# One fused two-block kernel: the attention modulation computed by quarters of the features instead of halves

## The chip, the cores and the metric

The kernel runs on one core of a Trainium2 chip. A core has a matrix engine (TensorE, called PE in the profile; PEld is its weight load), VectorE (DVE), ScalarE (ACT), GpSimd (POOL) and a queue processor that issues DMAs (SP). The metric is the device time of one execution in microseconds (us); the median of several runs counts.

## The reference

Two transformer blocks are computed for 256 tokens of 1024 features. The change lies in the first lines of the first block:

```
mod_x = silu(c)     @ w_ada + b_ada          # 1024 x 6144, one row for x
mod_c = silu(c_ctx) @ w_ada + b_ada          # and one for the context
sh_a, sc_a, g_a, sh_m, sc_m, g_m = split(mod_x, 6)      # the same for mod_c
hx = rmsnorm(x)   * (1 + sc_a)  + sh_a       # 256 x 1024
hc = rmsnorm(ctx) * (1 + csc_a) + csh_a      # 256 x 1024
qa, ka, va, qb, kb, vb, ga, gb = split(h @ w_in)        # for hx and for hc
```

Then come grouped-query and differential attention, an output merge, a mixture of 32 experts with 4 per token, and the second block (an mLSTM mixer, a MoBA attention mixer, and a feed-forward layer after each). Everything is float32.

## The kernel before

All weights come as one stream from HBM (`w_stream`), cut into tiles of 1 MB (128 partitions x 2048 numbers) in the order that `weight_plan` lists. SP issues the loads in that order; a load waits until one of five buffers (pool `w`) is free. A tile of `w_in` is split by `split` into two rounded parts, `whi` (ACT, L295) and `wlo` (DVE, L296), 128x1024 at a time; activations are split likewise (`hx_hi`, `hx_lo` for x, `hc_hi`, `hc_lo` for the context). A product of such parts is three PE instructions (`mm3`, L300 to L302).

The parts of `phase_a` that matter here, in the order of the code:

- `normed("x")` normalizes the token rows and transposes them on PE (L341).
- `modulation(half)` computes shift and scale of 512 of the 1024 features, for x and the context at once: 16 products (`ada_tile`, L504) of a stationary 128x32 block with `silu(c)` in column 0 and `silu(c_ctx)` in column 1. The scale goes to 32 rows of one PSUM bank and the shift to 32 others, so two 32-column groups of PE are in use; the sum over the eight 128-row blocks of `w_ada` is made in PSUM. ACT copies the result to `mod` (L619), PE transposes it (L511), and DVE adds the biases and the norm gain (L625 to L627).
- `modulated(n, k2)` applies it to two blocks of 128 features: one on DVE, one on POOL (L636), then ACT and DVE split the result.
- `first(n, ts, half)` is half of the contraction of the first projections: `vb` (512 columns) and `ka` (256 columns) for four tiles of 128 tokens, of which tiles 0 and 1 are x and 2 and 3 the context.

The sequence is: half 0 of the modulation, its products with x, the normalization of the context (`normed("ctx")`), products with the context, half 1, the rest. After these first products comes the block of `w_in` columns 1280 and up (`kb`), with the tiles of the later modulations (n = 1, 2) taken as a side task. A scheduler sets the final order of the instructions on each engine from the order of the code and the dependencies; each engine works through its own list in order.

Of the kernel before, what the change touches and what calls it, by code (L numbers as in the profile page):

```python
# [9 lines left out]
F32 = mybir.dt.float32  # L10
# [3 lines left out]
AF = mybir.ActivationFunctionType  # L14
OP = mybir.AluOpType
AX = mybir.AxisListType
PSUM = bass.MemoryType.PSUM

D = 1024
T = 256  # L20
KD = D // 128
# [36 lines left out]
def weight_plan():  # L58
# [4 lines left out]
    def add(name, layer, k0, kn, c0, n, split=True):  # L63
        plan.append((name, layer, k0, kn, c0, n, split))

    def ts(name, c0, n, ktot, layer=None, side=None, per=1):
        step = min(ktot, 2048 // n)
        for k0 in range(0, ktot, step):
            add(name, layer, k0, min(step, ktot - k0), c0, n)
            for _ in range(per if side else 0):  # L70
                add(*side.pop(0), False)
# [7 lines left out]
    def ada0(half):  # L79
        for k0 in range(0, KD, 2):  # L80
            add("w_ada", None, k0, 2, half * 1024, 1024, False)

    ada0(0)
    add("w_in", None, 0, 4, 1792, 512)
    ts("w_in", 512, 256, KD)
    ada0(1)
    add("w_in", None, 4, 4, 1792, 512)
    side = [("w_ada", None, k, 1, n * 2048, 2048) for n in (1, 2) for k in range(KD)]
# [148 lines left out]
class Kernel:  # L237
# [318 lines left out]
    def phase_a(self):  # L556
# [56 lines left out]
        def modulation(half):  # L613

            ps = self.pp.tile([128, 512], F32, name="ada", tag="ada", bufs=1)
            for k0 in range(0, KD, 2):
                self.ada_tile(ps, 64 * half, k0, 2, half * 1024, 1024)
            b = mod[64 * half:64 * half + 64]
            nc.scalar.activation(b, ps[64 * half:64 * half + 64], AF.Copy)  # L619
            mt = self.mod_T(mod, 64 * half, 64)  # L620
            cc = slice(4 * half, 4 * half + 4)
            wide = lambda v: v[:, None, :].to_broadcast([128, 2, 4])
            b0 = CR["b_ada"] + 4 * half
            g0 = CR["norm_attn"] + 4 * half
            nc.vector.tensor_add(sh[:, :, cc], mt[:, :, 32:34].rearrange("p c r -> p r c"), wide(self.cols[:, b0:b0 + 4]))  # L625
            nc.vector.tensor_tensor(sc[:, :, cc], mt[:, :, 0:2].rearrange("p c r -> p r c"), wide(b1[:, cc]), op=OP.add)
            nc.vector.tensor_tensor(sc[:, :, cc], sc[:, :, cc], wide(self.cols[:, g0:g0 + 4]), op=OP.mult)  # L627
# [20 lines left out]
        wf = {}  # L648
        def first(n, ts, half):

            for t in ts:
                o = bank_ka[t // 2][:, (t % 2) * 256:(t % 2 + 1) * 256] if n == "ka" else bank_vb[t]
                for k in range(4 * half, 4 * half + 4):
                    self.mm3(o, act(t)(k), wf[n](k if n == "ka" else k - 4 * half),
                             k == 0 and (n == "vb" or t % 2 == 0), k == KD - 1)
# [3 lines left out]
        modulated("x", 1)  # L659
# [3 lines left out]
        self.hp = hp  # L663
        wf["ka"] = w.take("w_in", None, 0, KD, 512, 256)
        bank_ka = [self.bank("psd") for _ in range(2)]
        normed("ctx")
        first("ka", (0, 1), 0)
        modulated("ctx", 0)
        modulated("ctx", 1)
        first("ka", (2, 3), 0)  # L670
        w.load(self.sv, a["k_sv"].rearrange("(o n) -> o n", o=1).to_broadcast([128, NSV]))
        modulation(1)
        first("vb", (2, 3), 0)
        modulated("x", 2)
        modulated("x", 3)
        modulated("ctx", 2)
        modulated("ctx", 3)
        wf["vb"] = w.take("w_in", None, 4, 4, 1792, 512)
        first("ka", range(4), 1)
        first("vb", range(4), 1)  # L680
# [1310 lines left out]
def pack(i):  # L1991

    f = lambda n: np.asarray(i[n])
    p = {}
# [28 lines left out]
    blocks = [2, 0, 3, 1] + list(range(4, 12))  # L2023
    w["w_ada"] = f("w_ada")[0].reshape(D, 12, 512)[:, blocks].reshape(D, 6 * D)
# [50 lines left out]
```

## Time and profile before

| | us |
|---|---|
| median of 3 runs | 1837.52 |
| lowest, highest | 1836.62, 1842.04 |
| profiled execution | 1840.18 |
| its span in the trace | 1838.40 |
| PE busy | 1751.6 (95%) |
| DVE busy | 792.8 (43%) |
| ACT busy | 533.1 (29%) |
| POOL busy | 123.2 (7%) |

The profile is of one execution; times in it count from the start of its span. "Busy" is time in which an engine has an instruction in hand. On PE the instructions are pipelined: a row lasts longer than the distance to the next start. A float32 product that is not split stands as two PE records, a product of split parts and a transpose as one.

### The profile page before, as it was taken

Reading aid. Unit: us, or ns where it says so; the run is one execution under the profiler, and the core shown is the slowest. Engines: PE = TensorE matmul, PEld = TensorE weight load, DVE = VectorE, ACT = ScalarE, POOL = GpSimd, SP = SyncE. Lnnn points to the kernel's source line nnn. Section 1 sums busy time; section 2 is a strip of 40 time slices with the busy share of each in tenths; the row PEclk is TensorE's granted clock in tenths of the full one; section 3 lists DMA queues with packets and bytes.
Section 4 is the critical chain, followed back from the end, with each engine's and each line's share of the span. In section 5 each row is a group of like instructions: output and inputs, shape, how many; then the busy total and the mean of one; then the engine's idle time right before and its main releaser. Section 6 shows DMA issues by size and latency. Waiting matters only on the chain.

```text
span 1838.4 us, 24331 instructions
## 1 busy us (share of the span) xinstructions
PE 1751.6 (95%) x9995; PEld 1106.0 (60%) x9995; DVE 792.8 (43%) x1596; ACT 533.1 (29%) x826; POOL 123.2 (7%) x167
## 2 busy tenths in 40 slices
PE   8999998999993999999989999889999999999999
PEld 4867895333331333333333333338999998899997
DVE  4688864222120121212211211136676657966653
ACT  3456741010100010101001001024554444655442
POOL 1320030000000000000000000010400002310000
PEclk9999998999997999999999999989999999999999
DMA  9475485999999999999999999994355554445551
GB/s 361 161 301 194 152 351 203 425 423 425 425 426 383 417 423 425 426 426 423 426 425 424 427 424 425 426 371 165 138 184 184 184 181 169 166 149 189 184 184 69
DMA packets 62903, 563.49 MB, mean 307 GB/s; under 512 B 8139, under 2 KB 8388, under 8 KB 10308
## 3 DMA queue, kind: packets, MB, share of 16 engines
q1 hardware_dynamic: 62096, 560.72, 75.9%
q8 instruction: 80, 1.31, 0.3%
q0 software_dynamic: 416, 1.05, 0.2%
q14 instruction: 35, 0.29, 0.0%
q10 hardware_dynamic: 276, 0.13, 0.0%
HBM read 560.82 MB, written 1.05 MB: 306 GB/s over the span
## 4 chain that ended last, share of the span: by engine, by line
PE 65%; DMA 30%; DVE 3%; ACT 1%; issue 1%; POOL 0%; ACTq 0%; SPq 0%; DVEq 0%
DMA w<-in_w_stream_dram 30%; PE bk L1415 18%; PE psd L300 12%; PE psd L301 12%; PE psd L302 12%; PE ada L504 2%; PE ps L1339 1%; PE ps L1380 1%; PE bk L1410 1%; DVE wlo L296 1%; PE psT L849 1%; PE bk L302 0%; PE bk L300 0%; PE bk L301 0%; PE ps L1443 0%
## 5 line engine op out<-in xcount | busy, mean ns | idle before, releaser
L1415 PE MATMUL bk<-w,xT 128*64 128x512 f32 x2048 | 500.8, 600 | 42.6 <-DMA w<-in_w_stream_dram 42.6
L296 DVE TENSOR_TENSOR wlo<-w,whi 128x1024 fp32r<-128x1024 f32 x246 | 298.9, 1240 | 138.2 <-ACT whi L295 135.0
L1415 PEld LDWEIGHTS bk<-w,xT 128*64 128x64 f32 x2048 | 152.1, 137 | 315.3 <-issue 263.3
L295 ACT ACTIVATE whi<-w 128x1024 fp32r<-128x1024 f32 x246 | 251.4, 1053 | 197.5 <-PE psd L301 110.6
L1415 PE MATMUL bk<-w,aT 128*64 128x512 f32 x1024 | 260.5, 606 | 12.3 <-DMA w<-in_w_stream_dram 11.6
L300 PE MATMUL psd<-u_hi,whi 128*128 128x256 f32 x768 | 217.2, 283 | 0.0
L302 PE MATMUL psd<-u_hi,wlo 128*128 128x256 f32 x768 | 215.3, 280 | 0.0
L301 PE MATMUL psd<-u_lo,whi 128*128 128x256 f32 x768 | 215.3, 280 | 0.0
L1415 PEld LDWEIGHTS bk<-w,aT 128*64 128x64 f32 x1024 | 79.3, 138 | 149.8 <-issue 125.2
L302 PEld LDWEIGHTS psd<-u_hi,wlo 128*128 128x128 f32 x768 | 146.9, 191 | 0.0
L301 PEld LDWEIGHTS psd<-u_lo,whi 128*128 128x128 f32 x768 | 144.3, 188 | 0.2
L300 PEld LDWEIGHTS psd<-u_hi,whi 128*128 128x128 f32 x768 | 144.2, 188 | 0.2
L1444 ACT ACTIVATE aT<-ps 128x512 f32<-128x512 f32 x32 | 19.1, 597 | 388.6 <-PE ps L1443 388.6
L1473 DVE TENSOR_SCALAR b_gate<-bk 128x512 f32<-128x512 f32 x32 | 20.6, 686 | 246.0 <-PE bk L1410 246.0
L1474 ACT ACTIVATE b_th<-b_gate 128x1024 f32<-128x1024 f32 x16 | 16.9, 1058 | 283.2 <-DVE b_gate L1473 283.2
L1433 DVE TENSOR_SCALAR sv<-bk 128x512 f32<-128x512 f32 x32 | 22.1, 692 | 176.2 <-PE bk L1410 176.2
L1403 DVE SCALAR_TENSOR_TENSOR y_lo<-bk,wc,y_hi 128x512 fp32r<-128x512 f32 x32 | 22.6, 747 | 138.7 <-ACT y_hi L1402 138.7
L1340 DVE SCALAR_TENSOR_TENSOR xT<-ps,g_m,xT 128x256 f32<-128x256 f32 x136 | 59.7, 479 | 43.2 <-PE ps L1339 43.2
L1402 ACT ACTIVATE y_hi<-bk,wc 128x512 fp32r<-128x512 f32 x32 | 20.3, 683 | 135.6 <-PE bk L1415 122.2
L1372 POOL TENSOR_TENSOR sw<-oh,wth 128x512 f32<-128x512 f32 x8 | 8.3, 1043 | 750.5 <-PE ps L1392 599.6
L1339 PEld LDWEIGHTS ps<-ohT,y_hi 128*128 128x128 f32 x128 | 23.8, 187 | 49.6 <-DVE xT L1340 27.8
L300 PE MATMUL psd<-whi,u_hi 128*128 128x512 f32 x128 | 52.5, 410 | 0.0
(510 smaller groups left out, 2789.2 us busy)
## 6 DMA issues: line engine op xcount, KB each, us to landing
w<-in_w_stream_dram SPq DMA_DIRECT2D x291, 1024.0 KB, 10.6
w<-in_w_stream_dram SPq DMA_DIRECT2D x119, 2048.0 KB, 28.0
w<-in_w_stream_dram SPq DMA_DIRECT2D x4, 512.0 KB, 4.5
x_rows<-in_x_dram SPq DMA_DIRECT2D x2, 512.0 KB, 4.4
vb<-in_ctx_dram SPq DMA_DIRECT2D x2, 512.0 KB, 15.3
out_dram<-x_rows SPq DMA_DIRECT2D x4, 256.0 KB, 2.0
sv<-in_k_sv_dram SPq DMA_DIRECT2D x1, 572.0 KB, 10.0
b_raw<-in_b_gate_dram POOLq DMA_DIRECT2D x2, 128.0 KB, 9.2
```

The source lines that it names most:

```text
L295: self.nc.scalar.activation(hi, v, AF.Copy)
L296: self.nc.vector.tensor_sub(lo, v, hi.bitcast(F32))
L300: mm(out, a[0], b[0], start=start, stop=False, skip_group_check=True)
L301: mm(out, a[0], b[1], start=False, stop=False, skip_group_check=True)
L302: mm(out, a[1], b[0], start=False, stop=stop, skip_group_check=True)
L504: self.nc.tensor.matmul(ps[p:p + 32, :], self.cs[:, k0 + k, :], v[:, k, j * 512:(j + 1) * 512], start=k0 + k == 0, stop=k0 + k == KD - 1, ...
L1339: self.nc.tensor.matmul(o, y[:, k * 128:(k + 1) * 128], places, start=i == 0, stop=i == len(terms) - 1)
L1340: self.nc.vector.scalar_tensor_tensor(self.xT[:, k, :], o, self.g_m[:, k:k + 1], self.xT[:, k, :], op0=OP.mult, op1=OP.add)
L1403: nc.vector.scalar_tensor_tensor(y[1][:, c], dn, wc, y[0][:, c].bitcast(F32), op0=OP.mult, op1=OP.subtract)
L1415: last = mm(o[64 * i:64 * i + 64], lhs[:, k, 64 * i:64 * i + 64], v[i], start=k == 0, stop=stop, skip_group_check=True)
L1433: nc.vector.tensor_scalar(u, o, 7.0, -7.0, op0=OP.min, op1=OP.max)
L1473: nc.vector.tensor_scalar(g[:, half(hf)], o[hf], 7.0, None, op0=OP.min)
```

## The change

The modulation is computed for 256 features at a time (four quarters). A quarter is two tiles of `w_ada` with 512 columns and four row blocks each, where the 512 columns are 256 of the shift followed by 256 of the scale. The four row blocks of a tile go to the four 32-column groups of PE, so the PSUM bank holds four partial sums of both rows. ACT copies the bank; four small products with a 128x2 matrix `pick` (ones in rows 0, 32, 64, 96 for its first column and 1, 33, 65, 97 for its second) add the four partial sums and transpose at once. The columns of `w_ada` in the stream are ordered to fit. `first` works by quarters too, and the code order changes: products with x for quarter 0, then quarter 1, the normalization of the context, quarters 0 and 1 with the context, quarter 2, quarter 3.

```diff
-    def ada0(half):
-        for k0 in range(0, KD, 2):
-            add("w_ada", None, k0, 2, half * 1024, 1024, False)
+    def ada0(q):
+        for k0 in (0, 4):
+            add("w_ada", None, k0, 4, q * 512, 512, False)
     ada0(0)
     add("w_in", None, 0, 4, 1792, 512)
+    ada0(1)
     ts("w_in", 512, 256, KD)
-    ada0(1)
+    ada0(2)
     add("w_in", None, 4, 4, 1792, 512)
+    ada0(3)
...
+        pick = long.tile([128, 2], F32, name="pick")
+        nc.vector.reduce_sum(pick, self.ident.rearrange("p (g s) -> p s g", s=32)[:, 0:2, :], axis=AX.X)
-        def modulation(half):
+        def modulation(q):
             ps = self.pp.tile([128, 512], F32, name="ada", tag="ada", bufs=1)
-            for k0 in range(0, KD, 2):
-                self.ada_tile(ps, 64 * half, k0, 2, half * 1024, 1024)
-            b = mod[64 * half:64 * half + 64]
-            nc.scalar.activation(b, ps[64 * half:64 * half + 64], AF.Copy)
-            mt = self.mod_T(mod, 64 * half, 64)
+            for k0 in (0, 4):
+                v = w.take("w_ada", None, k0, 4, q * 512, 512)
+                for k in range(4):
+                    nc.tensor.matmul(ps[32 * k:32 * k + 32, :], self.cs[:, k0 + k, :], v[:, k, :], start=k0 == 0,
+                                     stop=k0 == 4, skip_group_check=True)
+            nc.scalar.activation(mod, ps, AF.Copy)
+            for c in range(4):
+                nc.tensor.matmul(ps[:, 2 * c:2 * c + 2], mod[:, c * 128:(c + 1) * 128], pick, start=True, stop=True,
+                                 skip_group_check=True)
+            mt = ps[:, 0:8].rearrange("p (c r) -> p r c", r=2)
...
         modulation(0)
         modulated("x", 0)
-        modulated("x", 1)
         wf["vb"] = w.take("w_in", None, 0, 4, 1792, 512)
         first("vb", (0, 1), 0)
+        modulation(1)
+        modulated("x", 1)
+        first("vb", (0, 1), 1)
         wf["ka"] = w.take("w_in", None, 0, KD, 512, 256)
         normed("ctx")
-        first("ka", (0, 1), 0)
-        modulated("ctx", 0)
-        modulated("ctx", 1)
-        first("ka", (2, 3), 0)
-        modulation(1)
-        first("vb", (2, 3), 0)
+        for q in range(2):
+            first("ka", (0, 1), q)
+        for q in range(2):
+            modulated("ctx", q)
+            for n in ("vb", "ka"):
+                first(n, (2, 3), q)
+        modulation(2)
         modulated("x", 2)
+        modulated("ctx", 2)
+        first("ka", range(4), 2)
+        wf["vb"] = w.take("w_in", None, 4, 4, 1792, 512)
+        first("vb", range(4), 2)
+        modulation(3)
         modulated("x", 3)
-        modulated("ctx", 2)
         modulated("ctx", 3)
-        wf["vb"] = w.take("w_in", None, 4, 4, 1792, 512)
-        first("ka", range(4), 1)
-        first("vb", range(4), 1)
+        for n in ("vb", "ka"):
+            first(n, range(4), 3)
```

How the instructions stand on the engines is shown at three places. On ACT, before, from the copy of the first modulation (`mod`) to the second; `x_rows` with `vb` as source are the squares of the context rows:

```order
L619 ACTIVATE mod<-ada 64x512
L295 ACTIVATE whi<-w 128x1024
L295 ACTIVATE hx_hi<-h 128x512
L295 ACTIVATE whi<-w 128x1024
L295 ACTIVATE hx_hi<-h 128x512
L595 ACTIVATE x_rows_121,n_ss<-vb 128x1024 x2
L295 ACTIVATE whi<-w 128x1024 x2
L601 ACTIVATE ctx_nT<-psT 128x512 x4
L295 ACTIVATE hc_hi<-h 128x512 x2
L619 ACTIVATE mod<-ada 64x512
```

And the same place on ACT in the changed kernel (L297 is the old L295, L627 the old L619, L597 the old L595):

```order
L627 ACTIVATE mod<-ada 128x512
L297 ACTIVATE hx_hi<-h 128x512
L297 ACTIVATE whi<-w 128x1024 x2
L627 ACTIVATE mod<-ada 128x512
L597 ACTIVATE x_rows_121,n_ss<-vb 128x1024
L297 ACTIVATE hx_hi<-h 128x512
L597 ACTIVATE x_rows_121,n_ss<-vb 128x1024
L297 ACTIVATE whi<-w 128x1024 x2
L603 ACTIVATE ctx_nT<-psT 128x512 x4
L297 ACTIVATE hc_hi<-h 128x512 x2
```

The first `whi` has moved behind `hx_hi`, and the second modulation's copy and `hx_hi` now stand ahead of and between the squares of the context.

On PE in the changed kernel, around the modulation of quarter 1 (L625 its products, L630 the small ones; the product ahead is the last with quarter 0, those behind are the first with quarter 1):

```order
L304 MATMUL psd<-whi,hx_lo 128x512
L625 MATMUL ada<-w,cs 32x512 x8
L630 MATMUL ada<-pick,mod 128x2 x4
L302 MATMUL psd<-whi,hx_hi 128x512
L303 MATMUL psd<-wlo,hx_hi 128x512
L302 MATMUL psd<-whi,hx_hi 128x512
```

Nothing stands between the small products and the products that need their result. Before, 24 products with `hc` that do not need the second modulation stood behind its transposes.

On PE in the changed kernel, from the modulation of quarter 2 to the first products with it:

```order
L304 MATMUL psd<-whi,hc_lo 128x256
L625 MATMUL ada<-w,cs 32x512 x8
L630 MATMUL ada<-pick,mod 128x2 x4
L625 MATMUL ada<-w,cs 32x512 x5
L302 MATMUL psd<-whi,hx_hi 128x256
L303 MATMUL psd<-wlo,hx_hi 128x256
```

Five of the eight products of quarter 3 stand behind quarter 2's small products. The other three follow behind all products of quarter 2, and the small products of quarter 3 then stand between products of the `kb` block, of which 12 have moved ahead; the first tile of the next modulation (four products that stood together) is cut into one and three.

## Rows read from the trace of the kernel before

**Rows 1.** The page: PE's line of the busy times; the chain's shares.
```profile
PE 1751.6 (95%) x9995; PEld 1106.0 (60%) x9995; DVE 792.8 (43%) x1596; ACT 533.1 (29%) x826; POOL 123.2 (7%) x167
PE 65%; DMA 30%; DVE 3%; ACT 1%; issue 1%; POOL 0%; ACTq 0%; SPq 0%; DVEq 0%
```

**Rows 2.** Stretches: length, busy us (instructions) by engine, granted clock, DMA share, GB/s.
```profile
10.00:20.00 10.00, 10.00 (x48) 3.41 (x47) 2.81 (x5) 1.79 (x3) 0.00 (x0) 1.00 1.01 420
23.20:26.70 3.50, 3.48 (x9) 2.67 (x10) 3.40 (x6) 2.91 (x5) 1.44 (x1) 0.53 0.99 414
26.70:47.00 20.30, 19.38 (x118) 12.57 (x116) 8.09 (x25) 6.41 (x11) 1.26 (x2) 1.00 0.87 339
...
200.00:320.00 120.00, 114.57 (x825) 93.29 (x824) 72.74 (x209) 50.56 (x103) 16.57 (x27) 0.96 0.64 243
320.00:1240.00 920.00, 855.72 (x3737) 321.15 (x3735) 190.96 (x364) 93.77 (x151) 12.02 (x16) 0.98 1.00 420
```

**Rows 3.** Timeline, PE: start, us, instruction, count, [idle before, what ended it].
```profile
12.44 1.53 PE L341 MATMUL psT<-ident,x_rows 128*128 128x128 f32 x12
...
13.90 6.20 PE L504 MATMUL ada<-w,cs 128*32 128x512 f32 x26
...
23.22 1.09 PE L300 MATMUL psd<-whi,hx_hi 128*128 128x512 f32 x2 [1.98 <-ACT hx_hi L295]
```

**Rows 4.** Timeline, ACT, DVE and POOL, from the first modulation's copy on.
```profile
20.13 0.59 ACT L619 ACTIVATE mod<-ada 64x512 f32<-64x512 f32 x1 [5.53 <-PE ada L504]
20.62 1.04 ACT L295 ACTIVATE whi<-w 128x1024 fp32r<-128x1024 f32 x1
...
21.27 0.17 DVE L625 TENSOR_TENSOR sh_a<-ps,cols 128x8 f32<-128x8 f32 x1 [6.90 <-PE ps L511]
...
21.82 2.82 POOL L636 TENSOR_SCALAR h<-x_nT,sc_a,sh_a 128x256 f32<-128x256 f32 x2 [20.75 <-DVE sc_a L627]
22.53 0.63 ACT L295 ACTIVATE hx_hi<-h 128x512 fp32r<-128x512 f32 x1 [0.87 <-POOL h L636]
22.57 1.21 DVE L296 TENSOR_TENSOR wlo<-w,whi 128x1024 fp32r<-128x1024 f32 x1
```

**Rows 5.** Line L636: its POOL instructions, ns shortest/median/longest.
```profile
L636 POOL TENSOR_SCALAR h<-x_nT,sc_a,sh_a x4: 581/770/2147, 21.8 to 48.6; 128x256 f32<-128x256 f32 x4
```

**Rows 6.** Timeline, PE: part of the second modulation, and its transposes.
```profile
35.67 3.63 PE L504 MATMUL ada<-w,cs 128*32 128x512 f32 x16
...
46.60 0.46 PE L511 MATMUL ps<-ident,mod 64*128 64x64 f32 x4 [0.69 <-ACT mod L619]
```

**Rows 7.** Timeline, PE: one side tile of a later modulation, on four column groups.
```profile
80.82 1.06 PE L504 MATMUL ada<-w,cs 128*32 128x512 f32 x8
81.81 0.50 PE L300 MATMUL psd<-whi,hx_hi 128*128 128x512 f32 x1
```

**Rows 8.** Timeline, PE: float32 products with one moving column, and what follows.
```profile
282.49 1.93 PE L1125 MATMUL ps<-one,b_th 128*128 128x1 f32 x16
284.28 0.61 PE L1131 MATMUL ps<-eye,mod 128*128 128x32 f32 x4
```

**Rows 9.** Timeline, PE: 48 `ka` products from 52.69, 48 `vb` products from 58.44, `kb` block.
```profile
52.69 0.28 PE L300 MATMUL psd<-whi,hx_hi 128*128 128x256 f32 x1
...
58.44 0.40 PE L300 MATMUL psd<-whi,hx_hi 128*128 128x512 f32 x1
...
69.34 0.39 PE L300 MATMUL psd<-whi,hx_hi 128*128 128x512 f32 x1
```

**Rows 10.** Timeline, ACT and DVE: the second context rows' square, a split, their scaling.
```profile
26.37 1.06 ACT L595 ACTIVATE x_rows<-vb 128x1024 f32<-128x1024 f32 x1
...
30.13 2.36 DVE L296 TENSOR_TENSOR wlo<-w,whi 128x1024 fp32r<-128x1024 f32 x2 [0.27 <-issue]
...
32.59 0.75 DVE L597 TENSOR_SCALAR vb<-vb,n_r 128x1024 f32<-128x1024 f32 x1
```

**Rows 11.** Timeline, PE: the transposes of `kb`, in the stage behind the change.
```profile
116.41 0.66 PE L714 MATMUL psT<-ident,kb_row 128*128 128x128 f32 x4 [0.29 <-POOL kb_row L806]
```

More of the change, by code (lines that the diff above doesn't have):

```diff
@@ L611, in phase_a @@
         nc.vector.tensor_scalar(b1, self.cols[:, CR["b_ada"] + KD:CR["b_ada"] + 2 * KD], 1.0, None, op0=OP.add)
-        def modulation(half):
+        pick = long.tile([128, 2], F32, name="pick")
+        nc.vector.reduce_sum(pick, self.ident.rearrange("p (g s) -> p s g", s=32)[:, 0:2, :], axis=AX.X)
+        def modulation(q):
             ps = self.pp.tile([128, 512], F32, name="ada", tag="ada", bufs=1)
-            for k0 in range(0, KD, 2):
-                self.ada_tile(ps, 64 * half, k0, 2, half * 1024, 1024)
-            b = mod[64 * half:64 * half + 64]
-            nc.scalar.activation(b, ps[64 * half:64 * half + 64], AF.Copy)
-            mt = self.mod_T(mod, 64 * half, 64)
[L621 to L627, printed above, removed]
@@ new lines, in modulation @@
+            mt = ps[:, 0:8].rearrange("p (c r) -> p r c", r=2)
+            cc = slice(2 * q, 2 * q + 2)
+            wide = lambda v: v[:, None, :].to_broadcast([128, 2, 2])
+            b0 = CR["b_ada"] + 2 * q
+            g0 = CR["norm_attn"] + 2 * q
+            nc.vector.tensor_tensor(sc[:, :, cc], mt[:, :, 2:4], wide(b1[:, cc]), op=OP.add)
+            nc.vector.tensor_tensor(sc[:, :, cc], sc[:, :, cc], wide(self.cols[:, g0:g0 + 2]), op=OP.mult)
+            nc.vector.tensor_add(sh[:, :, cc], mt[:, :, 0:2], wide(self.cols[:, b0:b0 + 2]))
@@ L648, in phase_a, with first @@
         wf = {}
-        def first(n, ts, half):
+        def first(n, ts, q):
             for t in ts:
                 o = bank_ka[t // 2][:, (t % 2) * 256:(t % 2 + 1) * 256] if n == "ka" else bank_vb[t]
-                for k in range(4 * half, 4 * half + 4):
-                    self.mm3(o, act(t)(k), wf[n](k if n == "ka" else k - 4 * half),
+                for k in (2 * q, 2 * q + 1):
+                    self.mm3(o, act(t)(k), wf[n](k if n == "ka" else k % 4),
                              k == 0 and (n == "vb" or t % 2 == 0), k == KD - 1)
@@ L2021, in pack @@
     w["w_oa"] = f("w_oa").reshape(2, 4, 64, D).transpose(1, 0, 2, 3).reshape(512, D)
-    blocks = [2, 0, 3, 1] + list(range(4, 12))
-    w["w_ada"] = f("w_ada")[0].reshape(D, 12, 512)[:, blocks].reshape(D, 6 * D)
+    blocks = [0, 4, 1, 5, 2, 6, 3, 7] + list(range(8, 24))
+    w["w_ada"] = f("w_ada")[0].reshape(D, 24, 256)[:, blocks].reshape(D, 6 * D)
     p["k_tri"] = np.triu(np.ones((128, 128), np.float32), 1)
```

## The prediction

> **What bounds the kernel now.** I read the page's busy times and chain first: PE is busy 95% of the span and holds 65% of the chain, DMA 30% [rows 1]. Then the stretches: from 320 to 1240 us the DMA engines are full (share 1.00, 420 GB/s), while from 200 to 320 their share is only 0.64 [rows 2]. So the experts run at the pace of the DMA, but that stage begins when PE has worked through the attention: ahead of it the DMA waits for buffers that PE and the splits give back. A microsecond won or lost on PE in the first 70 us should reach the end whole.
>
> In those 70 us the change works between two points on PE: 13.9, when the transposes of x are done (12.44 + 1.53, [rows 3]; the same work stands ahead of this in both kernels), and 69.34, when the first products are done and the `kb` block begins [rows 9]. The 55.4 us between them are what the change can alter. The timeline shows how they pass now: modulation products to 20.1, a chain through ACT, PE, DVE, POOL and ACT, first product at 23.22 [rows 3, 4], half clock for the next 3.5 us (granted 0.53, that is 1.2 GHz for nearly all of it) [rows 2], then PE nearly without a pause.
>
> **Prices.** 48 products of 512 columns take 69.34 - 58.44 = 10.9 us, 0.23 each; 48 of 256 columns take 58.44 - 52.69 = 5.75, 0.12 each [rows 9]. On two column groups 16 records of the modulation take 3.6 us; on four, eight records take 81.81 - 80.82 = 0.99 [rows 6, 7]. A quarter's tile is exactly the latter: four products, 0.99 us at full clock. Eight tiles make 7.9 us, where before 64 records at 3.6 per 16 made 14.5.
>
> The four small products have no row of their own. From below: L511, four records in 0.46 [rows 6]. From above: L1125, float32 products with a 128x128 stationary block and one moving column, 16 records in 284.28 - 282.49 = 1.79, 0.112 per record; a float32 product is two records, so eight records are 0.9 [rows 8]. I take 0.9, since that row has the same operands.
>
> The Trainium skill ("TensorEngine Tiling (Array Packing)", Instruction Overhead) gives about 60 cycles of overhead per matmul and the same latency for 1 column as for 60. An estimate by that page at 2.4 GHz is 0.2 us for the eight records, which would make the sum below 2.8 us smaller; the row of L1125 shows over four times that, so I keep the row.
>
> **The walk on PE after the change.**
>
> Quarter 0: its second tile runs from 13.9 to 14.9. It is the second tile of the stream; before, the products went through four tiles from 13.9 on without waiting for one. ACT's copy takes 0.59, with its handover 0.65 (0.69 in [rows 6]): 15.55. Small products to 16.5. DVE's three additions and POOL's `h` start within 0.55 (21.27 to 21.82): 17.0; POOL 0.7 as in 21.82 to 22.53: 17.7; `hx_hi` [rows 4]. Here is a catch: `whi` (1.04) stood ahead of `hx_hi` and was free of the modulation; now it stands behind it on ACT, so PE waits until about 17.7 + 0.55 + 1.04 = 19.3. That is 3.9 us earlier than 23.22, not the 5.2 us by which the modulation itself ends earlier (20.1 to 14.9).
>
> Two of twelve products can run; the others need `wlo` (1.21 more): 20.5. PE has hardly worked since 14.9, a longer pause than the one before, and I let it fall to half clock for one stretch like that of [rows 2]: ten products at 0.43 or 0.23, done at 24.2.
>
> Quarter 1: two tiles, 26.2 (its tiles are fourth and fifth in the stream; `whi` at 20.62 already used the fifth before). Copy 0.65, small 0.9, chain 0.55 + 0.7 + 0.65 = 1.9: first product at 29.7. PE has nothing else in its list here, so it idles 2.55. Twelve products: 32.5.
>
> Context: the square of its second rows now stands behind quarter 1's `hx_hi` on ACT, so it ends near 30.8. From the end of that square (27.43) to the scaling (32.59), less the split of 2.36 that lay between, took 2.8; then 0.75 [rows 10]: 34.3. PE has four transposes (0.6) and waits 1.2; twelve more (1.5): 35.8.
>
> `ka` with x, 24 at 0.12: 38.7. Quarters 0 and 1 with the context, 24 of each size, 8.4: 47.1. Quarter 2: tiles 2.0, copy 0.65, small 0.9: 50.7. Its chain of 1.9 is mostly covered by five products of quarter 3 (0.99, and 0.86 for the fifth alone): 52.8. 48 products with quarter 2: 61.2. The three others of quarter 3, 0.9: 62.1. Copy and chain are covered by 12 products of `kb`, which I leave out on both sides. Small 0.9; the next side tile cut into one and three costs 0.86 + 0.9 for 0.99, so 0.8 more; 48 products, 8.4: 72.2.
>
> So the first products end at 72.2 instead of 69.34, +2.9. The same bookkeeping on the kernel before (7.2 us for the first 24 products, 24 and 48 at 0.12, 24 and 48 at 0.23, transposes 2.1, modulation 7.2 and its 1.1) gives about 69.0; it runs some 0.4 short. I forecast +3.4.
>
> Edits I price at nothing: `pick` on DVE (DVE waits for the constants there), the copy of 128 rows instead of 64 (the time goes with the columns), the smaller additions, SP's list (the same loads; each buffer comes free as early or earlier, and the DMA is full to 20 us and at 0.87 from 26.7 to 47 [rows 2]). About 14.3 MB up to the last modulation tile at 420 GB/s are 34 us, an estimate; it is needed at 51. If that cover went, PE would wait in quarter 3 a microsecond for each.
>
> **Bounds.** Small products at L511's price: -0.45 on four occasions, -1.8. No half clock at all: -1.4. POOL's `h` between 0.58 and 2.15 [rows 5]: up to +1.4 in quarter 0 or 1, where DVE is idle beside it, so I take 0.7. Half clock to the end of quarter 1's products: +0.7 on the first twelve, +2.0 on the tiles, +1.6 beyond the context's wait, +4.3 in all. Together 0 to about +9.
>
> **The rivals.**
>
> *Half clock through the whole of quarters 0 and 1 (slower).* PE pauses twice within 15 us (14.9 to 19.3 and 26.2 to 29.7, with only small products inside). For it: one pause of 3 us was enough before to bring 1.2 GHz [rows 2, 3]. Against it: the twelve products and two tiles between the pauses are 5 us of dense work. It decides if PE is still at 1.2 GHz at 24. Price +4.3: +7.7, 1845.2 us. The Trainium skill ("TensorE: Matmul & The Clock Gate", HAM oscillation) says that short bursts between waits make PE start each burst throttled; by that rule this rival holds.
>
> *The earlier start is kept (faster).* If the waits of quarters 1 and 2 and of the context vanished (2.55 + 0.65 + 1.2), with the low price of the small products and no half clock: 3.4 - 4.4 - 1.8 - 1.4 = -4.2, 1833.3 us. Against it: PE's list has nothing to put into those waits.
>
> *It does not reach the end.* If the DMA's full stretch began by itself, the shift would be absorbed: 0, 1837.5 us. Against it is the share of 0.64 before 320 us.
>
> *The four groups do not run together.* Then eight tiles cost some 6 us more. [Rows 7] speak against it.
>
> **How the numbers follow.** The profiled execution took 1840.18 us, 1.78 more than its span and 2.66 above the median of the runs. 1840.18 + 3.4 = 1843.6 in a profile like that one, and against the median 1837.5 + 3.4 = 1840.9. Chances: forecast 0.55, half clock 0.25, not reaching the end 0.11, earlier start kept 0.07, groups apart 0.02. A measurement of this kernel tells about 0.3% (5.5 us) from no change. The forecast by itself spans 1838.5 to 1843, all within that; slower by more needs the half clock or the groups apart and most of their price, 0.28; faster by more needs still more than the faster rival's sum, 0.05; same 0.67. The range reaches from a little below no change to just above the slow rival: 1835 to 1846.5.
>
> **What would show it.** Each tile's eight records in 0.99 us; eight records of small products in 0.9; first product near 19.3, behind `whi`; PE idle about 1.9 between quarter 1's small products and its first product; the context's transposes waiting for the scaling near 34; five and three products in quarter 3; the `kb` transposes [rows 11] at about 119.8 instead of 116.4, and the same shift when the DMA becomes full. A granted clock of 0.5 after 24 us speaks for the first rival. If the transposes come before 115, my walk misses work that fills the waits; if they come later but the end does not, the third rival holds.

## The result: slower by 9 us, and the profile after

The changed kernel takes 1848.32 us (median of 6 runs, 1847.21 to 1850.99), the kernel before 1839.15 in the same runs. The ratio is 1.0051 with an interval of 1.004 to 1.0063: slower by 0.5%, 1.8 us above the upper end of the predicted range. The profiled execution took 1850.99 us, its span 1849.2, 10.8 more than that of before. It came in portions (start of the instruction named; between `kb` and the second block the shift wanders from 7.8 up to 11.0 us at the end of the experts and comes back to 8.1, behind the last row norm it rises to 12.6 at 1770 us and falls again):

| on PE | before | after | shift |
|---|---|---|---|
| last transpose of x | 13.70 | 15.71 | 2.0 |
| first product | 23.22 | 21.67 | -1.5 |
| first transpose of `kb` | 111.91 | 119.67 | 7.8 |
| second block, first row norm | 1253.5 | 1261.6 | 8.1 |
| second block, last row norm | 1657.7 | 1669.5 | 11.8 |
| end of the span | 1838.4 | 1849.2 | 10.8 |

So 5.8 us were lost between the transposes of x and `kb`, where the prediction looked for the loss, 3.7 in a place that the change does not touch, and 2.0 ahead of the change.

The first place, PE in the changed kernel (start, duration, instruction, count, idle time before it and what ended it), which answers to [rows 3, 6, 11]:

```profile
14.45 1.53 PE L343 MATMUL psT<-ident,x_rows 128*128 128x128 f32 x12
15.91 1.07 PE L625 MATMUL ada<-w,cs 128*32 128x512 f32 x8
17.69 1.05 PE L630 MATMUL ada<-pick,mod 128*128 128x2 f32 x8 [0.72 <-ACT mod L627]
21.67 1.22 PE L302 MATMUL psd<-whi,hx_hi 128*128 128x512 f32 x2 [2.92 <-ACT whi L297]
...
27.14 1.92 PE L625 MATMUL ada<-w,cs 128*32 128x512 f32 x16
...
29.84 1.05 PE L630 MATMUL ada<-pick,mod 128*128 128x2 f32 x8 [0.78 <-ACT mod L627]
...
32.95 0.50 PE L302 MATMUL psd<-whi,hx_hi 128*128 128x512 f32 x1 [2.06 <-ACT hx_hi L297]
...
37.41 1.91 PE L343 MATMUL psT<-ident,vb 128*128 128x128 f32 x16
...
53.20 1.05 PE L630 MATMUL ada<-pick,mod 128*128 128x2 f32 x8 [0.72 <-ACT mod L627]
54.69 1.88 PE L625 MATMUL ada<-w,cs 128*32 128x512 f32 x10 [0.44 <-PE ada L630]
...
124.18 0.66 PE L732 MATMUL psT<-ident,kb_row 128*128 128x128 f32 x4 [0.27 <-POOL kb_row L824]
```

Each tile of the modulation is as short as forecast, and each of the first two quarters is followed by a pause of 2 to 3 us. A pause goes with a stretch at half clock, as the stretches show (length, busy us by engine, granted clock, DMA share, GB/s; compare [rows 2]):

```profile
21.60:26.70 5.10, 4.99 (x11) 3.50 (x12) 2.36 (x2) 0.96 (x2) 0.00 (x0) 0.50 0.96 394
26.70:33.00 6.30, 3.47 (x28) 1.52 (x26) 1.43 (x9) 2.36 (x5) 0.69 (x1) 1.00 0.86 317
33.00:36.90 3.90, 3.90 (x10) 3.10 (x11) 3.40 (x17) 2.83 (x4) 0.00 (x0) 0.56 0.85 349
36.90:50.00 13.10, 13.10 (x88) 11.85 (x87) 7.81 (x11) 5.37 (x9) 2.93 (x4) 1.00 0.45 162
```

Granted 0.50 is 1.2 GHz. The first group of 12 products began there; the second began at full clock and fell to half after two products, when PE had been at 2.4 GHz for some six microseconds in which it was busy for little more than half. The rest of the chain, on ACT, POOL and DVE, answers to [rows 4, 10]:

```profile
17.04 0.60 ACT L627 ACTIVATE mod<-ada 128x512 f32<-128x512 f32 x1 [0.43 <-PE ada L625]
...
19.32 0.68 POOL L648 TENSOR_SCALAR h<-x_nT,sc_a,sh_a 128x256 f32<-128x256 f32 x1 [18.25 <-DVE sc_a L638]
20.04 0.63 ACT L297 ACTIVATE hx_hi<-h 128x512 fp32r<-128x512 f32 x1 [2.40 <-POOL h L648]
20.57 1.99 ACT L297 ACTIVATE whi<-w 128x1024 fp32r<-128x1024 f32 x2
...
32.27 0.63 ACT L297 ACTIVATE hx_hi<-h 128x512 fp32r<-128x512 f32 x1 [1.44 <-DVE n_r_v L313]
...
32.81 1.04 ACT L597 ACTIVATE x_rows<-vb 128x1024 f32<-128x1024 f32 x1
...
36.80 0.75 DVE L599 TENSOR_SCALAR vb<-vb,n_r 128x1024 f32<-128x1024 f32 x1
```

`whi` stands behind `hx_hi`, and the second square of the context behind quarter 1's `hx_hi`, as the order said. PE's transposes of the context, from 37.41 on, did not wait for this scaling.

The second place, in the second block. The row norms (shortest, median, longest in ns, then first and last start) in the kernel before, then in the changed one:

```profile
L445 PE MATMUL ps<-r_diag,one x6: 378/378/378, 1253.5 to 1657.7; 128*128 128x256 f32 x6
```

```profile
L447 PE MATMUL ps<-r_diag,one x6: 377/378/379, 1261.6 to 1669.5; 128*128 128x256 f32 x6
```

And 50 us of PE work without a gap in that part, again before and after, columns as in the stretches above:

```profile
1480.00:1530.00 50.00, 50.00 (x425) 50.00 (x424) 26.96 (x27) 19.98 (x24) 2.33 (x3) 1.00 0.53 183
```

```profile
1480.00:1530.00 50.00, 50.00 (x419) 50.00 (x419) 27.91 (x29) 21.03 (x25) 2.34 (x3) 1.00 0.48 171
```

PE is busy all the time at full clock in both, and yet it starts 419 products instead of 425: one per 119.3 ns instead of 117.6. Nothing waits; the same work runs 1.4% slower, and from the first row norm to the last it takes 407.9 us instead of 404.2.

### The profile page after: what moved, and what is told of

Same layout as the page of the kernel before. It is cut to its first block, busy times and chain, and to the rows that moved or that the text cites. A ratio compares the mean times of both kernels' runs of the same rounds, so it can differ in the third digit from the quotient of the medians.

```text
span 1849.2 us, 24393 instructions
## 1 busy us (share of the span) xinstructions
PE 1757.2 (95%) x10019; PEld 1111.3 (60%) x10019; DVE 794.2 (43%) x1603; ACT 534.5 (29%) x828; POOL 120.1 (6%) x167
## 3 DMA queue, kind: packets, MB, share of 16 engines
q0 software_dynamic: 416, 1.05, 0.2%
HBM read 560.82 MB, written 1.05 MB: 304 GB/s over the span
## 4 chain that ended last, share of the span: by engine, by line
PE 70%; DMA 27%; DVE 2%; ACT 1%; issue 1%; POOL 0%; ACTq 0%; SPq 0%; DVEq 0%; POOLq 0%
DMA w<-in_w_stream_dram 26%; PE bk L1433 20%; PE psd L302 13%; PE psd L303 12%; PE psd L304 12%; PE ps L1357 2%; PE ps L1398 1%; PE ada L506 1%; PE bk L1428 1%; PE psT L867 1%; PE ps L1461 0%; PE ada L625 0%; PE bk L304 0%; PE bk L302 0%; PE yps L896 0%
## 5 line engine op out<-in xcount | busy, mean ns | idle before, releaser
L297 ACT ACTIVATE whi<-w 128x1024 fp32r<-128x1024 f32 x246 | 251.4, 1053 | 200.4 <-PE psd L303 116.0
L302 PE MATMUL psd<-whi,u_hi 128*128 128x512 f32 x128 | 52.8, 413 | 0.0
```

Of the source, the lines that this page charges most:

```text
L297: self.nc.scalar.activation(hi, v, AF.Copy)
L302: mm(out, a[0], b[0], start=start, stop=False, skip_group_check=True)
```

## The experiments

All times are medians, ratios are to the kernel before in the same runs. Its medians there went from 1836.5 to 1840.2 us, so rows are compared by their ratios. "To `kb`" is the time on PE from the last transpose of x to the first one of `kb`, "block 2" the time from the first to the last row norm of the second block; both are of the profile.

| kernel | us | ratio (interval) | to `kb` | block 2 |
|---|---|---|---|---|
| before, first profile | 1839.15 | 1 | 98.2 | 404.2 |
| before, again | 1837.62 | 1.0004 (0.9995 to 1.0013) | 98.2 | 404.4 |
| changed, first | 1848.32 | 1.0051 (1.004 to 1.0063) | 104.0 | 407.9 |
| changed, again | 1846.89 | 1.0055 (1.004 to 1.0069) | 104.0 | 408.0 |
| pauses filled | 1849.05 | 1.0064 (1.0052 to 1.0076) | 103.5 | 409.4 |
| quarter 1 early | 1842.44 | 1.0033 (1.0021 to 1.0044) | 98.6 | 408.0 |
| before, moved by 32 B | 1843.22 | 1.0026 (1.0017 to 1.0036) | 97.8 | 409.4 |
| changed, ones in free columns | 1845.94 | 1.0044 (1.0028 to 1.0061) | 104.0 | 404.1 |
| the same, quarter 1 early | 1839.56 | 0.9997 (0.9988 to 1.0006) | 97.3 | 404.3 |
| the same, split of `w_in` first | 1845.08 | 1.0025 (1.0016 to 1.0034) | 103.2 | 404.2 |
| four groups, order of before | 1837.25 | 0.9991 (0.998 to 1.0003) | 96.6 | 405.8 |
| put together | 1836.46 | 0.9982 (0.9973 to 0.9991) | 93.9 | 404.2 |
| put together, again | 1836.68 | 0.9985 (0.9976 to 0.9994) | 93.9 | 405.7 |
| before, moved by 64 B | 1845.38 | 1.0035 (1.0022 to 1.0049) | 97.7 | 408.2 |
| before, moved by 128 B | 1845.33 | 1.0033 (1.0024 to 1.0043) | 97.8 | 407.3 |
| before, moved by 512 B | 1840.04 (1 run) | | 97.9 | 404.2 |
| before, moved by 1024 B | 1839.18 (1 run) | | 97.9 | 404.3 |

In four rows block 2 holds 1.5 to 1.6 us that are not of the edit: in pauses filled, before moved by 32 B, four groups, and put together again, PE falls to half clock behind a wait of 1.5 to 1.6 us for a split, near 1555 us; the wait stands in the others too, the half clock does not (put together: granted 0.50 from 1548.6 to 1552.0 in the second profile, 1.00 throughout there in the first). And the part from `kb` to the second block takes from 1138.1 to 1142.6 us in the 17 profiles, 1141.6 and 1140.4 in the two of before, so a single profile's span says little about an edit of 2 us.

**Both kernels once more** (no edit).

> The kernel before, once more, with a new profile. Theory A (the 2.0 us by which the changed kernel's profile is late already when the transposes of x are done, 15.98 instead of 13.97, belong to one execution: a landing of the first constants 0.94 us later, and two products at half clock, 1.07): this profile has its own value there, somewhere between 13 and 16 us. Theory B (they belong to the change): 13.97 within 0.2 again. Both: kb block's transposes at the same distance from there as in the first profile, 111.91 - 13.70 = 98.2, within 0.7. Time within 0.3% of the kernel before.

> The changed kernel, once more, with a new profile. Theory A (start of one execution): the transposes of x end anywhere between 13 and 16 us, and the rest from there to the kb transposes takes 119.67 - 15.71 = 104.0 again, 5.8 more than before, within 0.7. Theory B: 15.98 again. In both the two stretches at half clock (12 products with quarter 0, 10 with quarter 1) come again. Time 7 to 11 us above the kernel before.

The transposes of x ended at 14.47 and 15.35, so the start has a value of its own in each execution, as theory A says; but in the seven profiles with the order by quarters it is 14.93 on the mean, in the ten others 14.04. In six of the seven the first constants (`crows`) land 0.5 us later behind the identity, 1.0 to 1.2 instead of 0.5 to 0.6 us; in the seventh they do not, though its instructions there are the same, and one of the ten has 0.9. What decides it stays open. Both longer stretches came again to 0.1 us: 98.2 and 104.0 to `kb`, 404 and 408 in block 2. They belong to the kernels.

**The two pauses filled.** The fillers are 128-column products of the identity, written to a bank that is overwritten later:

```
+        def warm(n, b):
+            for _ in range(n):
+                nc.tensor.matmul(bank_vb[3][:, 0:128], b[:, 0:128], self.ident, start=True, stop=True, skip_group_check=True)
...
+            if q < 2:
+                warm((3, 0)[q], self.ident)
             nc.scalar.activation(mod, ps, AF.Copy)
...
+            if q < 2:
+                warm((12, 8)[q], mod)
```

> The changed kernel with products of the identity put into the pauses of quarters 0 and 1 (3 and 12 in the first, 8 in the second), written to a bank that is overwritten later. Clock theory (what is lost is the half clock behind each pause): the products with quarter 0 run at full clock and take 2.8 us instead of 5.1, those of quarter 1 3.0 instead of 4.5; the context's squares stand behind quarter 1 and move with it; kb transposes 2.5 to 3.5 us earlier than in the changed kernel, and the time lower by as much. Waiting theory (the chain through quarter 1's copy, its split and the context's normalization sets the time whatever PE's clock is): first transposes of the context at the same time within 1 us, time the same within 1.5 us. If the fillers themselves hold PE up, it is slower by up to 2 us.

The clock theory got its clock and not its time. The stretches of this kernel, columns as above:

```profile
21.00:27.00 6.00, 5.31 (x30) 2.52 (x28) 2.36 (x2) 1.16 (x2) 0.00 (x0) 1.00 0.99 406
30.80:34.00 3.20, 3.12 (x14) 2.32 (x15) 2.78 (x13) 2.96 (x5) 0.00 (x0) 1.00 0.98 411
48.00:51.00 3.00, 2.28 (x21) 0.64 (x19) 0.00 (x0) 0.60 (x1) 0.00 (x0) 1.00 0.19 22
51.00:57.00 6.00, 5.56 (x27) 2.89 (x28) 3.62 (x8) 2.12 (x3) 1.39 (x2) 0.72 0.98 403
```

Both groups of 12 products ran at full clock, and the first transpose of the context came 3.0 us earlier, counted from the transposes of x. By the first product with the context 1.6 of that was left, since the second half of the transposes then waited 1.1 us for the scaling. Then a half clock came that the changed kernel had not had, behind the small products of quarter 2 (granted 0.72), and by `kb` 0.5 was left. So the half clock costs what the products take longer, but of the 3.0 us that its absence gained, the next wait took back about 1.4 and the new half clock 1.1.

**Quarter 1's modulation in the first pause.** Only the first products with x move behind it:

```
-        first("vb", (0, 1), 0)
         self.hp = hp
         modulation(1)
+        with self.tc.issue_after(self.last_ada.ins):
+            first("vb", (0, 1), 0)
         modulated("x", 1)
```

> The changed kernel with one thing moved: the products of the modulation of quarter 1 stand in the pause behind quarter 0's small products, ahead of the first products with x. Waiting theory (the loss is the two pauses that each quarter's own chain brings): quarter 1's eight products take 2.1 us of the 2.9 us pause, its chain runs beside the 12 products with quarter 0, the second pause (2.05 us, and 0.8 ahead of the small products) goes, and the context's normalization on ACT, which stands behind quarter 1, starts 5 us earlier: kb transposes 4 to 6 us earlier than in the changed kernel, time lower by as much. Clock theory: the same if PE stays at full clock in the shorter pause, and 2.5 us of it lost if not. If the loss lies in quarters 2 and 3 or in the start, less than 2 us.

PE in this kernel:

```profile
16.38 1.05 PE L630 MATMUL ada<-pick,mod 128*128 128x2 f32 x8 [0.72 <-ACT mod L627]
17.88 1.07 PE L625 MATMUL ada<-w,cs 128*32 128x512 f32 x8 [0.44 <-PE ada L630]
19.28 1.07 PE L625 MATMUL ada<-w,cs 128*32 128x512 f32 x8 [0.34 <-DMA w<-in_w_stream_dram]
20.36 0.49 PE L302 MATMUL psd<-whi,hx_hi 128*128 128x512 f32 x1
21.62 0.50 PE L303 MATMUL psd<-wlo,hx_hi 128*128 128x512 f32 x1 [0.77 <-DVE wlo L298]
```

The pauses of 2.92, 0.78 and 2.06 us are gone, 0.44, 0.34 and 0.77 stand in their place, and 98.6 us to `kb` instead of 104.0 are 5.4 of the 5.8. The half clock was not avoided (0.74 from 21.5 to 28, 0.72 from 45 to 51). The time fell by 4 us (1842.4 against 1846.9), so 6 remain over the kernel before, though `kb` comes only 0.4 us later than there, counted from the transposes of x. The waiting theory holds for the first place; the rest lies elsewhere.

**The tile of 8 bytes.** The matrix of ones, `pick`, is a tile in the pool that stays open through the attention. In the layout of the program it takes 32 bytes a partition, and some 100 tile names behind it stand 32 bytes further than before, among them the activations of the second block: `u_lo` and `u_hi` (79,520 and 87,712 before; 79,552 and 87,744) and `f_lo` and `f_hi` (103,104 and 125,632 before), whose products fill nearly all of the 50 us above. The weight parts `whi` and `wlo` of that block stay where they were. One kernel has the move without the change (first edit, to the kernel before), one the change without the move (second, to the changed kernel):

```
         b1 = long.tile([128, KD], F32, name="b1")
+        pad = long.tile([128, 2], F32, name="pad")
+        nc.vector.memset(pad, 0.0)
```

```
-        pick = long.tile([128, 2], F32, name="pick")
+        pick = self.cols[:, 124:126]
```

> The kernel before, with nothing but a tile of 128x2 numbers more in the pool that stays open through the attention (written once by DVE, never read). It stands where the changed kernel has its matrix of ones and moves the tiles behind it in memory by 32 bytes a partition, as there. Address theory (in both profiles of the changed kernel the stretch from the second block's first row norm to its last, 404.3 us in both profiles of before, takes 408.0, its 256-column products 0.118 to 0.120 us apart instead of 0.1165 to 0.118; this comes from the 32 bytes): this stretch takes 408.0 here too, the stretch from the expert sort to its last use 84.2 instead of 83.3, c_tanh starts 1.1 us behind the landing of the identity instead of 0.6, and the time is 3 to 5 us above the kernel before. Theory that these belong to the changed order or the changed modulation: 404.3, 83.3, 0.6, and a time within 1 us of before.

> The changed kernel with its matrix of ones put into two free columns of a tile that is there anyway, so that every later tile has the address that it has before the change. Address theory: second block 404.3 us instead of 408.0, and a time 3 to 5 us below the changed kernel, so that about 5.5 to 7 us remain over the kernel before: the 5.8 us between the transposes of x and the kb block, and what clock or start give. Theory that the address has no part: the same time as the changed kernel, 10 us above before. In both the two pauses and the half clock of quarters 0 and 1 stay.

The same 50 us, of before with the move, then of the change without it:

```profile
1480.00:1530.00 50.00, 50.00 (x419) 50.00 (x418) 26.68 (x27) 19.88 (x23) 2.33 (x3) 1.00 0.52 180
```

```profile
1480.00:1530.00 50.00, 50.00 (x425) 50.00 (x424) 26.00 (x26) 19.90 (x23) 2.33 (x3) 1.00 0.52 184
```

The 32 bytes alone make the kernel before slower by 0.26% (3 to 7 us), with 419 products; without them the changed kernel has 425 again, with the same instructions in the same order. In the time of the runs the changed kernel gains less than expected by this, 1.0055 to 1.0044, which the intervals do not tell from none; with quarter 1 early, below, it is 1.0033 to 0.9997. Part of what the move costs in block 2 comes back behind it: from the last row norm to the end it is 179.7 us in all five profiles moved by 32 bytes and 180.7 or 180.8 in those at the addresses of before (two executions aside, of which the last section tells), so that 2.7 of the 3.7 us reach the end. Two parts of the address theory fell: neither c_tanh's distance (0.50 and 1.14 us) nor the stretch after the expert sort (83.1 and 84.2) follows the address. The latter is 1 us, and PE's half clock around 300 us lasts longer there.

**How far must the tiles move?** The same edit with tiles of 16, 32, 128 and 256 numbers.

> The kernel before with a tile of 16 numbers more in the long-lived pool instead of 2, so that the tiles behind it move by 64 bytes a partition instead of 32. If the 32 bytes matter because of the place within 64 bytes: the second block's stretch takes 404.3 us again (409.4 with 32 bytes), its 256-column products 0.1165 us apart from 1290 to 1330, and the time is within 1.5 us of before. If any move of the tiles costs: 408 to 410 and 3 to 4 us above before, as with 32 bytes.

> The kernel before with a tile of 32 numbers more: the tiles behind it move by 128 bytes a partition. If the cost has a period of 128 bytes: second block 404.3 us, products from 1290 to 1330 at 0.1165 us. If any move costs (the layout of before is a lucky one): 408 us or more, 0.118 or more, time 3 to 6 us above before.

> The same with 512 bytes. Period of 512 or a part of it: 404.3 us and 0.1165. Any move costs: 408 or more.

> The same with 1024 bytes. Period of 1024 or a part of it: 404.3 us and 0.1165. Any move costs: 408 or more.

Moved by 128 bytes, then by 512:

```profile
1480.00:1530.00 50.00, 50.00 (x419) 50.00 (x418) 26.45 (x26) 19.90 (x23) 2.34 (x3) 1.00 0.53 181
```

```profile
1480.00:1530.00 50.00, 50.00 (x425) 50.00 (x424) 26.84 (x27) 19.89 (x23) 2.33 (x3) 1.00 0.53 182
```

My guess of 64 bytes was wrong: 64 and 128 cost as much as 32 (at 64 other stretches are the slow ones: 427 starts in these 50 us, but 419 from 1370 to 1420, where before has 426). 512 and 1024 cost nothing: 404.2 and 404.3 us in block 2 (the times are of one run each). So if the effect has a period, it divides 512; whether it is 512 or 256 was not tried, nor which of the moved tiles matter and against which others.

**One part of the change alone: four groups, in the order of before.** Two quarters at a time, the second with a bank and a copy of its own, the ones in free columns:

```
+        mod2 = pn.tile([128, 512], F32, name="mod2")
         def modulation(half):
+            for i in range(2):
+                quarter(2 * half + i, (mod, mod2)[i],
+                        self.bank("ada") if i else self.pp.tile([128, 512], F32, name="ada", tag="ada", bufs=1))
```

> One part of the change alone, in the order of the kernel before: the modulation on four column groups with the small products, two quarters at a time (each with a bank and a copy of its own), so that half 0 and half 1 stand where they stood; the matrix of ones in free columns, so the addresses move no tile by 32 bytes. If the form of the modulation is cheap and the order by quarters is what costs: half 0's last chain ends about where it did (the split of w_in now stands behind both splits of x on ACT, first product 23 to 24 us), half 1 takes about 4.1 + 2.1 us instead of 7.2 + 0.5, so 1.5 less, and the time is 0 to 3 us below the kernel before. If the form itself costs (small products of 1.06 us instead of 0.46 for each quarter, copies waited for): 2 to 5 us above before.

The form of the modulation is not what costs: 96.6 us to `kb` against 98.2, and a time 1.8 us lower, which the interval does not tell from none. PE shows why it is not more:

```profile
16.18 1.05 PE L633 MATMUL ada<-cols,mod 128*128 128x2 f32 x8 [0.72 <-ACT mod L630]
17.16 1.92 PE L628 MATMUL ada<-w,cs 128*32 128x512 f32 x16
19.80 1.05 PE L633 MATMUL ada<-cols,mod 128*128 128x2 f32 x8 [0.72 <-ACT mod L630]
23.86 0.82 PE L301 MATMUL psd<-whi,hx_hi 128*128 128x512 f32 x2 [3.00 <-ACT whi L296]
```

The modulation of the half ends its work on PE at 20.9, but the order puts `whi` behind both `hx_hi` on ACT, and the first product starts at 23.86.

**Both causes taken out, and the wait for `whi`.** The first is quarter 1 early with the ones in free columns. In the second the ones are in free columns, quarter 1 stands where the change put it, and one line of the order is forced, `modulated("x", 0)` behind the first half of the split:

```
-        modulated("x", 0)
         wf["vb"] = w.take("w_in", None, 0, 4, 1792, 512)
+        with self.tc.issue_after(self.first_hi.ins):
+            modulated("x", 0)
```

> The changed kernel with both: the modulation of quarter 1 in the pause behind quarter 0's small products, and the matrix of ones in free columns. If address (3 to 4 us) and pauses (5.4 us, from the trace with quarter 1 early) are separate causes and add up: first products and kb transposes as in the run with quarter 1 early (98.6 us from the transposes of x to the kb block), second block 404.3 us, time 1843 - 3.5, that is 0 to 3 us above the kernel before. If they do not add up: 4 us or more above it.

> The changed kernel with the matrix of ones in free columns and one order forced: on ACT the first half of the split of w_in stands ahead of hx_hi of quarter 0, as before the change. The prediction counted 1.04 us for whi behind hx_hi, on the way to the first product. If that holds: first product 0.95 us earlier (5.0 us behind the last transpose of x instead of 5.97), the products with quarter 0 at half clock all the same, and the kb transposes about 0.9 us earlier; time 0 to 2 us below that with the ones in free columns alone. If what follows (half clock to a fixed time, or the context's chain) takes it back: same kb transposes within 0.3 us.

With both causes out the changed kernel takes as long as the kernel before (0.9997): its 9 us are accounted for together. The single steps do not add up (4.4 us for the pauses alone, 2.0 for the ones alone, 10.6 together, from 1.0055 to 0.9997), with intervals of 2 to 3 us each. Some of the rest is the clock: with both out PE has one stretch at half clock up to `kb`, with quarter 1 early alone it had two, and `kb` comes 1.3 us sooner (97.3 against 98.6).

With the split of `w_in` first, `kb` comes 0.8 us sooner (103.2 against 104.0), near the 0.9 expected, but not in the way expected: the first product stands 6.1 us behind the last transpose of x, where it stood at 6.0, and not at 5.0. These are the rows, on PE, POOL and DVE:

```profile
20.33 0.93 PE L305 MATMUL psd<-whi,hx_hi 128*128 128x512 f32 x2 [3.03 <-ACT hx_hi L299]
17.88 1.74 POOL L651 TENSOR_SCALAR h<-x_nT,sc_a,sh_a 128x256 f32<-128x256 f32 x1 [16.81 <-DVE sc_a L641]
18.13 1.22 DVE L300 TENSOR_TENSOR wlo<-w,whi 128x1024 fp32r<-128x1024 f32 x1
```

POOL's `h` took 1.74 us with DVE's split beside it, where it took 0.68 in the changed kernel with DVE's split later, and that used up the microsecond that `whi` no longer took. The gain comes behind it: `wlo` is there when the first products run, and the 0.76 us that PE's weight load waited for it in the changed kernel are gone. What `whi` alone is worth was not shown.

**A version put together.** The order by halves and the four groups, `w_in`'s first tile third in the stream, its first split ahead of `hx_hi`, and quarter 1's products ahead of the first products (an excerpt; the modulation itself is as in the four groups above):

```
     ada0(0)
     add("w_in", None, 0, 4, 1792, 512)
+    ada0(1)
     ts("w_in", 512, 256, KD)
...
         modulation(0)
+        ada_q1 = self.last_ada
+        with self.tc.issue_after(self.vb_hi.ins):
+            modulated("x", 0)
         modulated("x", 1)
+        with self.tc.issue_after(ada_q1.ins):
+            first("vb", (0, 1), 0)
```

> A version put together from what the runs showed: the order of the kernel before (halves), the modulation on four column groups; quarter 1's products directly behind quarter 0's small products in a bank of their own, ahead of the first products; w_in's first tile third in the stream as in the changed kernel, its first split ahead of hx_hi; the ones in free columns. From the transposes of x on: one tile 1.0, copy 0.7, small 1.06, two tiles 2.06: 19.2 to 19.5 us, where the first product can start at once (24.0 before), then 12 products and the small ones of quarter 1 to 23.3, whose chain ends there too: PE has no pause over 1 us. 24 products end near 26 us instead of 31.4, the context's transposes end near 31 instead of 35.5, half 1 takes 1.5 us less: kb transposes 5 to 6.5 us earlier than before, 92 to 93 us behind the transposes of x instead of 98.2. Time 4 to 7 us below the kernel before if no half clock comes later; 2 to 4 if one does.

> The version put together, once more, with a new profile (the first one was its fastest execution, 1831.3 against a median of 1836.5). If its gain is that of the first 110 us: kb transposes 93 to 95 us behind the transposes of x again (93.9; 98.2 before), the rest of the program as long as in before's profiles within what executions differ, time 3 to 5 us below the kernel before. If the gain was of one execution: 97 us or more.

```profile
14.07 1.06 PE L634 MATMUL ada<-w,cs 128*32 128x512 f32 x8
15.85 1.05 PE L639 MATMUL ada<-cols,mod 128*128 128x2 f32 x8 [0.72 <-ACT mod L636]
16.83 1.06 PE L634 MATMUL ada<-w,cs 128*32 128x512 f32 x8
18.77 1.06 PE L634 MATMUL ada<-w,cs 128*32 128x512 f32 x8 [0.87 <-DMA w<-in_w_stream_dram]
19.93 0.50 PE L304 MATMUL psd<-whi,hx_hi 128*128 128x512 f32 x1
```

It beats both kernels: 0.9982 and 0.9985, about 3 us below before (1 to 5 by the intervals), with 93.9 us to `kb` in both profiles. That is a little less than the 92 to 93 us and the 4 to 7 us expected. The longest pause of PE on the way is now 0.87 us (1.0 in the second profile), for a tile that has not landed. The clock:

```profile
14.00:28.00 14.00, 11.99 (x71) 7.05 (x69) 9.14 (x32) 8.93 (x14) 2.43 (x2) 1.00 1.02 418
28.00:48.00 20.00, 19.36 (x133) 14.06 (x131) 8.66 (x22) 6.11 (x12) 5.20 (x8) 1.00 0.94 377
```

PE stays at full clock up to `kb`, where the kernel before had one stretch at half and the changed one two.

## Why the prediction was wrong, point by point

- **Its picture of the bound held.** The 5.8 us that arose by `kb` stood to the end (7.8 at `kb`, 8.1 at the second block), so the rival that it does not reach the end is out, and the full DMA stretch began later too (share 0.99 from 305 to 310 us before, 0.01 after, 0.92 from 315 on).
- **The walk had the right mechanism and too small a size**: +2.9 (+3.4 with its margin) against +5.8. Up to quarter 0's chain it is right: the first product stands 5.7 us behind the transposes of x where the walk had 5.4. Small products take 1.05 a quarter to the end of the last, for which the chain waits, instead of 0.9; where other products follow at once, those start after 0.8. The 12 products with quarter 0 took 5.5 us instead of 4.9. Those with quarter 1 took 4.5 instead of 2.8: that is the step "twelve products: 32.5", and with it the second half-clock stretch. Of that, 1.2 us took the place of a wait for the context's scaling that the walk had and that did not come, and the transposes took 1.7 instead of 2.1: at the end of `ka` with x PE was 1.25 us behind the walk (26.05 us from the transposes of x instead of 24.8). Another 0.4 is quarter 3's tile waiting until DVE had read quarter 2's small products from the one bank (read by 54.6, tile at 54.69), a wait that the walk did not have. Rest tiles, cuts and small products of quarters 2 and 3 make up the remaining 1.1: 61.1 us instead of 58.3 from the transposes of x to the end of the first products, the 12 `kb` products among them taken off. The sums have small slips of their own: 50.7 and a chain of 1.9 make 52.6, not 52.8, and the bookkeeping of before names 72 products of 256 columns where its 69.0 needs the 96 that there are.
- **The rival of the half clock was half right.** Both groups ran mostly at half clock (granted 0.50 and 0.56), as it said, but the clock had risen for quarter 1's tiles in between. The rule of the Trainium skill ("TensorE: Matmul & The Clock Gate", HAM oscillation), that bursts between waits start throttled, agrees with the first of these two stretches; in the second the clock fell 0.56 us into the burst, and behind the wait of 1.5 to 1.6 us near 1555 us it fell in four profiles of 17. The rival's price of +4.3 does not hold: filling both pauses brought both groups to full clock and gained 0.5 us at `kb`, with a new stretch at half clock later. The pauses cost by themselves: quarter 1's products in the first of them gained 5.4 with half clock still there. That the rival's +7.7 is nearer the measured +9.2 than the forecast is no sign for it, since 2.7 us came from the layout, which it did not have.
- **The step that failed is "Edits I price at nothing: `pick` on DVE".** Its work costs nothing, its place in memory does: 3.7 us in block 2, 2.7 at the end. With the ones in free columns the changed kernel took 1845.94 us, inside the range. The term of the walk that was mis-sized most is "twelve products: 32.5", 4.5 us instead of 2.8. The four groups, the order and the waits were weighed; the layout of the tiles behind the new one was not looked at.
- **The same work stands ahead of the transposes of x**, as the prediction said, but they end 2.0 us later in this profile. 0.9 us of that (mean of the seven profiles with the order by quarters against the ten others) have no explanation here; the rest lies within the scatter of single executions, 13.7 to 15.7 us in all profiles.

Together: 5.8 + 3.7 + 2.0 - 0.7 (+0.3 from `kb` to the second block, -1.0 behind the last row norm) make the 10.8 of the two profiles.

## What to carry to other kernels

Cutting a stage into pieces gives each piece the whole chain behind it (copy, small products, additions, splits: 4.7 and 3.9 us here); here it paid when the next piece's work stood in that chain's pause, so look first at what the order puts between a piece and its consumer. After any change that adds a tile, compare the addresses of the tiles behind it, and if the tile must be new, put it into free columns of an old one, as was done here, or last, which was not tried. Where the shift grows in a part that was not changed, count instructions per stretch of unbroken work before looking for a wait.

## What the runs showed of the hardware

The distance between products of 256 columns at full clock without any wait depended on where the tiles lie: at the addresses of before, or moved by 512 or 1024 bytes, it is 117.6 ns from 1480 to 1530 us (in the second profile of the version put together this work is over before 1530, and up to there it runs at the same pace); moved by 32 or 128 bytes it is 119.0 to 119.3 there, and moved by 64 it is 119.3 from 1370 to 1420, where before has 117.1 to 117.4. Whether it is PE's own reads that slow down, or something that the other moved tiles do to them, was not tried. Something else shows in two single executions at the old addresses: from about 1690 us on, 50 us hold 444 starts instead of 427 (113 ns a product), in the first profile of the version put together and in that of the split first, each the fastest of its runs. So the end of one profile can differ by 4 us from the next with no difference in the program behind it, and the medians have to be asked. Both stretches stand here, of the version put together, first and second profile:

```profile
1690.00:1740.00 50.00, 50.00 (x444) 50.00 (x443) 33.47 (x37) 22.72 (x26) 0.00 (x0) 1.00 0.54 190
```

```profile
1690.00:1740.00 50.00, 50.00 (x427) 50.00 (x427) 31.59 (x36) 22.34 (x27) 0.00 (x0) 1.00 0.52 184
```
